# Two blocks in fp32 on one core: slabs of memory on two sets of PSUM banks, the second half of the queries in four steps, and the first layer's memory normalised under the output projection

## The chip, the core and the metric

The kernel runs on one core of one Trainium2 chip, in one launch. The time is device microseconds (us) from the start of the launch to its end, the median of three runs. The engines of the core are TensorE (matmuls, with a separate row PEld for its weight loads), VectorE (DVE), ScalarE (ACT), GpSimd (POOL) and SyncE (SP); each works off its own list of instructions in order. SP's list holds nearly all DMAs, so a DMA that waits for a buffer holds back the DMAs behind it. Matmuls write to PSUM, which has eight banks of 128 x 512 fp32.

## The reference

All tensors are fp32; there are S = 512 positions, a model width of 1024, and 256 rows of memory. Two blocks of two layers each run one after the other. Cut to what the change touches:

```python
for l in range(2):                                   # first block
    mix = concat(diff_attn, mla, sliding_window)(rmsnorm(x, g_mix_pre[l]) @ w_in[l]) @ w_out[l]
    x = x + rmsnorm(mix, g_mix_post[l])
    mem_n = rmsnorm(mem, g_x_mem[l])                 # 256 x 1024
    q = rmsnorm(x, g_x_pre[l]) @ w_xq[l]             # 512 x 1024, four heads of 256
    k, v = split(mem_n @ w_xkv[l], 2)                # 256 x 1024 each
    x = x + rmsnorm(softmax(q k^T / 16) v @ w_xo[l], g_x_post[l])
    x = x + rmsnorm((silu(gate) * up) @ w_ffn_out[l], g_ffn_post[l])

mem_n = rms_norm(mem_2, mem_norm_g)                  # second block, one memory for both layers
for l in range(2):
    x = x + (attention_and_rglru if l == 0 else pool_mixer)(rms_norm(x, mix_norm_g[l]))
    q = rms_norm(rms_norm(x, xattn_norm_g[l]) @ xa_w_q[l], q_g)       # per head of 256
    k, v = split(mem_n @ xa_w_kv[l], 2);  k = rms_norm(k, k_g)
    x = x + softmax(q k^T / 16) v @ xa_w_o[l]
    x = x + square(relu(rms_norm(x, mlp_norm_g[l]) @ mlp_w1[l])) @ mlp_w2[l]
```

## The kernel before

Every fp32 operand is kept as two tiles, H (rounded to the fp32r type) and L (the rest, in the same type), and every product is three matmuls: H by H, H by L, L by H (`three`). Weights come by DMA in chunks of 512 KB into one of three `raw` buffers, ScalarE makes wH and VectorE wL from it (L373, L374 or L371, L429), into a pool `wp` of ten buffers; five chunks fit. Activations are normalised row block by row block: squares and sum on ScalarE (L380), the reciprocal root on POOL, the scaling on VectorE (L406) and ScalarE (L408), four transposes on TensorE (L411) and the split into actH (L347) and actL (L354).

A projection is worked off in slabs of 512 columns. `slab_B` computes rows by columns (tiles pB), `slab_A` the transposed result (tiles pA). A slab takes a named set of PSUM banks: "mm" is the two banks of the pool mm; "A" is mm, mm, tp, tp; "B" is sc, sc, sc, ob; "E", "F" and "K" are other mixtures. The pools hold 2 (mm), 3 (sc), 2 (tp) and 1 (ob) banks, eight in all. A slab's first matmul into a bank waits until the bank's last contents have been read out.

Memory has two row blocks, so a slab of memory needs two banks. Keys are made by `k_first` in the first block (four slabs of 256 columns, one for each head, L371 writes ko) and by `k_second` in the second (two slabs of 512 columns; `head_norm` reads them out: two squares on ScalarE at L832, POOL, two scalings into kn on VectorE at L836; then transposes ktr at L814). Values come from `mem_v`, two slabs (tiles vo). All of them are on "mm". Keys and values go to DRAM and are loaded head by head (xk, xv, L780 and L781) into buffers of `wp`.

The memory of each layer of the first block, and the one memory of the second block, is normalised early by `mem_norm` into tiles memH and memL of the ring r4, stored to DRAM (memd) and loaded again later by `mem_again`. For the first layer this happens in the stage of the input projections (`mem_norm(mem_raw(I["mem"][0]), "xmem0", split[0])`); the tiles are loaded again behind a `hold` on POOL while the attention heads of the layer end, and the output projection w_out (`out_postnorm`, tiles pB from mixH) comes between the reload and `k_first`.

`cross_heads` runs four heads with four units each, one per row block: scores xs on a bank of sc, a maximum on VectorE, the exponential xp on ScalarE (L862), its scaling, two transposes xtr (L869), the split into xpt, and after the fourth unit the outputs xo. In the second block (`second_rest`) the queries are made in two halves of 512 columns; the first half is a slab on "A" ahead of head 0, the second a slab on "B" that `make_q(1)` issues behind unit (0, 1). `make_q` also transposes the queries of its head (ytr, read out into yq).

The order on each engine is set by the tile framework's scheduler, which replays the program with its own costs and places each instruction when its inputs, a buffer and its engine are due; the program order decides between instructions that are ready. So a change in banks or in program order moves instructions over some tens of microseconds around it.

Of the kernel before, what the change touches and what calls it, by code (L numbers as in the profile page):

```python
# [10 lines left out]
F32 = mybir.dt.float32  # L11
# [6 lines left out]
P = 128  # L18
# [136 lines left out]
def two_blocks(ctx: ExitStack, tc: tile.TileContext, I, out):  # L155
# [261 lines left out]
    split = [None]  # L417
    gate = [None]

    def load_chunk(pieces, nk=2, ncols=512, gain=None):  # L420
# [9 lines left out]
        for a in range(nk):  # L430
            split[0] = put_hl(H[:, a], L[:, a], raw[:, a],
                              gain=None if gain is None else gain[:, a:a + 1],
                              copy=gain is not None)
# [325 lines left out]
    def mem_v(act, wkv, vd, tag, halves=(0, 1), t_outer=False, vnew=None):  # L759
        for hf in halves:  # L760
# [14 lines left out]
            slab_B(cols_of(wkv, [(D + hf * 512, D + hf * 512 + 512)]), act, ev, tag, t_outer=t_outer)  # L775
# [9 lines left out]
    def k_first(act, wkv, kv, new, tag="mm"):  # L785
        kd, vd = kv
        for h in range(4):
# [5 lines left out]
            slab_A(cols_of(wkv, [(h * 256, h * 256 + 256)], nk=4), act, ev, tag)  # L793

    def k_second(act, wkv, l, kv, new, tag="mm"):
# [6 lines left out]
        for hf in range(2):  # L802
# [4 lines left out]
            slab_B(cols_of(wkv, [(hf * 512, hf * 512 + 512)]), act, ev, tag)  # L807
# [31 lines left out]
    def cross_heads(make_q, q, kv, kvh, oT, otag="ob"):  # L839
# [6 lines left out]

        def unit(h, t):
            if t == 0 and h + 1 < 4:
                kvh[h + 1] = kv_load(kv, h + 1)
# [110 lines left out]
    def first_layer(l, act, cq, xsrc, nxt_gain, spill, mact, kv, nxt_mem, small):  # L960
# [34 lines left out]
        if mact is None:  # L995
            mact = mem_norm(mem_raw(I["mem"][0]), "xmem0", split[0])

# [358 lines left out]
        mact = mem_again(mact, pt2, marks[(2, 0)])  # L1356
# [14 lines left out]
        mem_v(mact, I["w_xkv"][l], kv[1], "mm")  # L1371
# [76 lines left out]
    def even_layer(act, mact, kv, small):  # L1448
# [133 lines left out]
        mem_v(mact, I["xa_w_kv_2"][0], kv[1], "mm")  # L1582
# [188 lines left out]
```

## Time and profile before

| | us |
|---|---|
| median of 3 runs | 2866.86 (2866.78 to 2867.74) |
| the profiled execution | 2867.16 |
| its span | 2865.4 |
| TensorE busy | 2819.8 (98%) |
| VectorE busy | 1484.6 (52%) |
| ScalarE busy | 1302.0 (45%) |
| GpSimd busy | 206.8 (7%) |

333.56 MB go through the DMAs in the span, 116 GB/s on the mean; 33.16 MB of it are written. The busy time of TensorE counts a matmul from its start to a modelled end, and matmuls overlap; a small idle share can therefore hide in it, and a matmul that takes longer than its like counts as busy as well. How TensorE stands in one stretch is read from its waits, from the granted clock of the stretch, and from the starts of single matmuls.

### The profile page before, as it was taken

To read this page: it belongs to the slowest core of one execution; us is meant where nothing else is said; L and a number is where in the kernel's file an instruction comes from. 1 tells how busy PE (TensorE), PEld (TensorE's weight loads), DVE (VectorE), ACT (ScalarE), POOL (GpSimd) and SP (SyncE) were. 2 spreads that over 40 slices of the span, in tenths; PEclk is the share of its full clock that TensorE was granted. 3 is DMA by queue.
4 is the path that set the end of the run, shared out by engine and by line. 5 is a ranking of instruction groups with operands and counts; after the bars stand their busy time and mean duration, and the time that the engine had idled before them with its cause. 6 is when DMAs were issued, how large, how long until landed. Compare 5 with 4: busy or idle time off the path is not lost.

```text
span 2865.4 us, 39327 instructions
## 1 busy us (share of the span) xinstructions
PE 2819.8 (98%) x14816; PEld 2376.8 (83%) x14816; DVE 1484.6 (52%) x2940; ACT 1302.0 (45%) x2656; POOL 206.8 (7%) x573
## 2 busy tenths in 40 slices
PE   8999999999999999999999999999999999999999
PEld 7868888888898778888888878888888878888887
DVE  7695554334366856543344765555334454554443
ACT  6584444333366745443333664444223344443222
POOL 2121000000011210000000210100000001000000
PEclk9999999999999999999999999999999999999999
DMA  6424633334252345333342523533332353232332
GB/s 206 130 81 138 213 111 96 98 97 131 94 171 88 89 133 184 104 103 97 99 130 95 155 68 119 167 126 97 101 96 96 119 177 110 67 110 96 96 96 74
DMA packets 235645, 333.56 MB, mean 116 GB/s; under 512 B 14656, under 2 KB 135872, under 8 KB 235456
## 3 DMA queue, kind: packets, MB, share of 16 engines
q1 hardware_dynamic: 234880, 328.96, 36.0%
q8 instruction: 116, 1.90, 0.3%
q10 hardware_dynamic: 576, 2.10, 0.2%
q14 instruction: 73, 0.60, 0.1%
HBM read 297.84 MB, written 33.16 MB: 116 GB/s over the span
## 4 chain that ended last, share of the span: by engine, by line
PE 90%; DVE 4%; ACT 4%; issue 1%; DMA 1%; POOL 1%; POOLq 0%; ACTq 0%; DVEq 0%; SPq 0%
PE pB L224 40%; PE pA L224 38%; PE xs L224 2%; PE xo L224 1%; ACT wH L373 1%; PE tr L411 1%; PE ms L224 1%; PE at L1109 1%; ACT h L380 1%; DVE wL L374 1%; PE sws L224 1%; PE mo L224 1%; PE swt L1177 1%; DVE dp L1206 1%; PE dfo L224 1%
## 5 line engine op out<-in xcount | busy, mean ns | idle before, releaser
L374 DVE SCALAR_TENSOR_TENSOR wL<-raw,par,wH 128x512 fp32r<-128x512 f32 (+2 forms) x696 | 436.9, 672 | 505.1 <-ACT wH L373 498.6
L373 ACT ACTIVATE wH<-raw,par 128x512 fp32r<-128x512 f32 (+2 forms) x696 | 417.2, 655 | 592.3 <-issue 216.4
L224 PE MATMUL pA<-actL,wH 128*128 128x512 f32 (+1 forms) x1808 | 650.1, 360 | 0.9 <-DVE actL L354 0.9
L224 PE MATMUL pA<-actH,wH 128*128 128x512 f32 (+1 forms) x1808 | 648.3, 361 | 2.6 <-ACT wH L373 1.5
L224 PE MATMUL pA<-actH,wL 128*128 128x512 f32 (+1 forms) x1808 | 648.0, 360 | 0.4 <-DVE wL L374 0.4
L224 PEld LDWEIGHTS pA<-actH,wH 128*128 128x128 f32 x1808 | 340.6, 189 | 54.8 <-ACT actH L347 1.8
L224 PEld LDWEIGHTS pA<-actH,wL 128*128 128x128 f32 x1808 | 341.5, 189 | 51.0 <-DVE wL L374 0.7
L224 PEld LDWEIGHTS pA<-actL,wH 128*128 128x128 f32 x1808 | 341.9, 189 | 50.4 <-DVE actL L354 1.5
L371 DVE TENSOR_TENSOR wL<-raw,wH 128x512 fp32r<-128x512 f32 (+1 forms) x334 | 215.2, 685 | 324.3 <-ACT wH L429 315.4
L429 ACT CAST wH<-raw 128x1024 fp32r<-128x1024 f32 (+1 forms) x168 | 175.5, 1045 | 338.6 <-PE pB L224 160.5
L224 PE MATMUL pB<-wL,mH 128*128 128x512 f32 x512 | 199.2, 389 | 0.0
L224 PE MATMUL pB<-wH,mH 128*128 128x512 f32 x512 | 198.8, 389 | 0.0
L224 PE MATMUL pB<-wH,mL 128*128 128x512 f32 x512 | 198.8, 389 | 0.0
L224 PE MATMUL pB<-wH,actH 128*128 128x512 f32 (+2 forms) x416 | 143.4, 349 | 2.2 <-ACT xp L862 1.5
L224 PE MATMUL pB<-wL,actH 128*128 128x512 f32 (+2 forms) x416 | 144.2, 347 | 0.4 <-DVE wL L374 0.4
L224 PE MATMUL pB<-wH,actL 128*128 128x512 f32 (+2 forms) x416 | 144.0, 347 | 0.0
L224 PE MATMUL pB<-wL,fH 128*128 128x512 f32 x352 | 137.5, 391 | 0.0
L224 PE MATMUL pB<-wH,fL 128*128 128x512 f32 x352 | 136.5, 390 | 0.0
L224 PE MATMUL pB<-wH,fH 128*128 128x512 f32 x352 | 136.2, 390 | 0.0
L224 PEld LDWEIGHTS pB<-wH,mH 128*128 128x128 f32 x512 | 96.1, 188 | 20.1
L224 PEld LDWEIGHTS pB<-wH,mL 128*128 128x128 f32 x512 | 96.1, 188 | 20.0
L224 PEld LDWEIGHTS pB<-wL,mH 128*128 128x128 f32 x512 | 96.1, 188 | 19.8
(361 smaller groups left out, 4666.4 us busy)
## 6 DMA issues: line engine op xcount, KB each, us to landing
raw<-in_mlp_w SPq DMA_DIRECT2D x128, 512.0 KB, 3.7
raw<-in_w_ffn_in SPq DMA_DIRECT2D x176, 256.0 KB, 3.2
raw<-in_w_ffn_out SPq DMA_DIRECT2D x44, 512.0 KB, 3.4
raw<-in_w_xkv SPq DMA_DIRECT2D x32, 512.0 KB, 4.1
raw<-in_xa_w_kv SPq DMA_DIRECT2D x32, 512.0 KB, 4.4
raw<-in_ev_w_in SPq DMA_DIRECT2D x20, 512.0 KB, 3.7
raw<-in_w_in SPq DMA_DIRECT2D x16, 512.0 KB, 4.9
raw<-in_w_out SPq DMA_DIRECT2D x16, 512.0 KB, 3.6
```

The source lines that it names most:

```text
L224: nc.tensor.matmul(o, a, b, start=start, stop=stop_)
L371: nc.vector.tensor_tensor(out=l, in0=src, in1=h.bitcast(F32), op=ALU.subtract)
L373: i = nc.scalar.activation(h, src, AF.Copy, scale=gain)
L374: nc.vector.scalar_tensor_tensor(out=l, in0=src, scalar=gain, in1=h.bitcast(F32), op0=ALU.mult, op1=ALU.subtract)
L380: nc.scalar.activation(junk, src, AF.Square, scale=1.0 / 32.0, accum_out=ssq[:, hf:hf + 1])
L411: nc.tensor.transpose(pt[:, i * P:(i + 1) * P], h[j][:, i * P:(i + 1) * P], ident)
L429: nc.scalar.copy(H, raw)
L1109: nc.tensor.transpose(tp[:, i * P:(i + 1) * P], src[:, i * P:(i + 1) * P], ident)
L1177: nc.tensor.transpose(tp[:, i * P:(i + 1) * P], pr[i][:, kt * P:(kt + 1) * P], ident)
L1206: nc.vector.tensor_tensor_reduce(out=pm[m], in0=sc, in1=ndt[t], scale=-DIFF_SLOPES[h], scalar=BIG, op0=ALU.add, op1=ALU.min, accum_out=nmx)
```

## The change

There are three parts. First, slabs of memory alternate between the sets "mm" and "B": the heads of `k_first`, the halves of `k_second`, and the halves of `mem_v` where both are made together (in the last layer each half of the values is still alone, on "mm").

Second, the first layer's memory is no longer normalised among the input projections. Its two raw tiles of 512 KB are loaded behind a `hold` on the marker at which the reload stood before, and `mem_norm` writes the normalised halves straight into tiles of the pool ptp (`new=pt2`). There is no copy in DRAM for this layer: four writes of 512 KB and eight reads of 256 KB go. A tile of ptp holds two column blocks instead of four, so the split takes four instructions per row block on ScalarE and four on VectorE instead of two and two with the double size, as before on reloading. The other two memories keep their way through DRAM. The helper that tied the first memory's squares to a weight conversion (`split`, `issue_after`) goes.

Third, the second half of the queries in the second block is issued in four steps of 24 matmuls on "mm": the first two row blocks over chunks 0 and 1, then over chunks 2 and 3, then the other two row blocks over the same chunks, which stay in `wp` until then. One step follows each unit of head 0. The keys and values of head 1 are loaded in unit (0, 3) instead of (0, 0).

```diff
-    def mem_raw(memrow):
+    def mem_raw(memrow, after=None):
         ms = [r4([P, D], F32, "memraw") for _ in range(MEM // P)]
         for t, m in enumerate(ms):
+            hold(m, after)
             nc.sync.dma_start(out=m, in_=memrow[t * P:(t + 1) * P, :])
         return ms

-    def mem_norm(ms, name, after=None):
-
-        act = Act(8, MEM, "mem", gain=pr(name), new=r4)
+    def mem_norm(ms, name, new=r4):
+
+        act = Act(8, MEM, "mem", gain=pr(name), new=new)
         for t, m in enumerate(ms):
-            h = [hbuf([P, S], F32, "h") for _ in range(2)]
-            ssq = sm(3, "ssq")
-            with tc.issue_after(after) if after is not None else nullcontext():
-                sq_halves(m, h, ssq)
-            prenorm_tile(m, act, t, "tp", ssq, h)
+            prenorm_tile(m, act, t, "tp")
+        if new is not r4:
+            return act
         act.copy = drp.tile([2, 8, P, MEM], F32, name=nm("memd"))
...
-            slab_B(cols_of(wkv, [(D + hf * 512, D + hf * 512 + 512)]), act, ev, tag, t_outer=t_outer)
+            slab_B(cols_of(wkv, [(D + hf * 512, D + hf * 512 + 512)]), act, ev,
+                   ("mm", "B")[hf] if len(halves) == 2 else "mm", t_outer=t_outer)
...
-            slab_A(cols_of(wkv, [(h * 256, h * 256 + 256)], nk=4), act, ev, tag)
+            slab_A(cols_of(wkv, [(h * 256, h * 256 + 256)], nk=4), act, ev, ("mm", "B")[h % 2])
...
-            slab_B(cols_of(wkv, [(hf * 512, hf * 512 + 512)]), act, ev, tag)
+            slab_B(cols_of(wkv, [(hf * 512, hf * 512 + 512)]), act, ev, ("mm", "B")[hf])
...
-            if t == 0 and h + 1 < 4:
+            if t == (3 if parts and h == 0 else 0) and h + 1 < 4:
                 kvh[h + 1] = kv_load(kv, h + 1)
...
                 for t in range(NT):
                     yield unit(h, t)
+                    if h == 0 and parts:
+                        yield piece(parts[t])
                     if t == 1 and h + 1 < 4:
                         yield filler(h + 1)
...
-        if mact is None:
-            mact = mem_norm(mem_raw(I["mem"][0]), "xmem0", split[0])
-
...
-        mact = mem_again(mact, pt2, marks[(2, 0)])
+        if mact is None:
+            mact = mem_norm(mem_raw(I["mem"][0], marks[(2, 0)]), "xmem0", pt2)
+        else:
+            mact = mem_again(mact, pt2, marks[(2, 0)])
         load_x(xsrc, marks[(2, 2)])
...
+        def quarters():
+
+            nrm = nrms[1] = [r2([P, S], F32, "yn") for _ in range(NT)]
+            src, n = cols_of(wq, [(512, 1024)])
+            ch, banks = {}, {}
+
+            def step(p, c):
+                if c == 0:
+                    banks[p] = banks_of("mm", 2, "pB")
+                for kc in (2 * c, 2 * c + 1):
+                    if kc not in ch:
+                        ch[kc] = src(kc, act2.gain)
+                    H, L = ch[kc]
+                    for i in range(2):
...
+                            three(banks[p][i], H[:, k2, :], L[:, k2, :], act2.h(k, *ts),
+                                  act2.l(k, *ts), k == 0, k == act2.nk - 1, False)
+                if c == 1:
+                    for i in range(2):
+                        head_norm(banks[p][i], nrm[2 * p + i], 2, 256)
+
+            return [lambda p=p, c=c: step(p, c) for p in range(2) for c in range(2)]
+
         def make_q(h):
             hf = h // 2
-            if h < 2:
-                slab_q(h)
+            if h == 0:
+                slab_q(0)
...
-        cross_heads(make_q, q, kv, kvh, oT, "mm")
+        cross_heads(make_q, q, kv, kvh, oT, "mm", quarters())
```

Three places show what this does to the order. On TensorE, at the keys of the last layer (`k_second`), the list before has these rows; pB_21374 and pB_21375 are the two banks of the first half of the keys, pB_21474 is the first bank of the second half, and ktr is the transposed first half:

```order
L224 MATMUL pB_21375<-wH_21438,memH_21040 128x512
L224 MATMUL pB_21375<-wL_21439,memH_21040 128x512
L224 MATMUL pB_21375<-wH_21438,memL_21041 128x512
L814 MATMUL ktr_21574<-csb,kn_21370 128x128
L224 MATMUL pB_21474<-wH_21478,memH_21038 128x512
L224 MATMUL pB_21474<-wL_21479,memH_21038 128x512
L224 MATMUL pB_21474<-wH_21478,memL_21039 128x512
```
and the changed list, where pB_21359 and pB_21360 are the first half and pB_21459 the first bank of the second:

```order
L224 MATMUL pB_21360<-wH_21423,memH_21025 128x512
L224 MATMUL pB_21360<-wL_21424,memH_21025 128x512
L224 MATMUL pB_21360<-wH_21423,memL_21026 128x512
L224 MATMUL pB_21459<-wH_21463,memH_21023 128x512
L224 MATMUL pB_21459<-wL_21464,memH_21023 128x512
L224 MATMUL pB_21459<-wH_21463,memL_21024 128x512
L224 MATMUL pB_21459<-wH_21463,memH_21023 128x512
```
Before, a transpose of the first half's keys stands between the halves, and the second half begins in a bank of the same pair. Now the second half begins right behind the first, in other banks; its 48 matmuls follow without a break and the transposes come behind them.

On TensorE, at head 0 of the cross attention of the second block's first layer, before (ytr are query transposes, xs the scores of one row block each, pB the second half of the queries on four banks, of which pB_17895 is the first):

```order
L1668 MATMUL ytr_17843<-csb,yn_17663 128x128
L1668 MATMUL ytr_17843<-csb,yn_17664 128x128
L1668 MATMUL ytr_17843<-csb,yn_17665 128x128
L224 MATMUL xs_17856<-xk_17658,yq_17834 128x256 x2
L224 MATMUL xs_17871<-xk_17658,yq_17834 128x256 x2
L224 MATMUL pB_17895<-wH_17901,actH_17090 128x512
L224 MATMUL pB_17895<-wL_17902,actH_17090 128x512
L224 MATMUL pB_17895<-wH_17901,actL_17091 128x512
```
and now (pB_17857 is the second of the two banks of the first row blocks, and wH_17940 the last weight chunk):

```order
L224 MATMUL pB_17857<-wH_17940,actH_17077 128x512
L224 MATMUL pB_17857<-wL_17941,actH_17077 128x512
L224 MATMUL pB_17857<-wH_17940,actL_17078 128x512
L224 MATMUL xs_17841<-xk_17643,yq_17823 128x256 x2
L224 MATMUL xs_17903<-xk_17643,yq_17823 128x256 x2
L224 MATMUL xs_17999<-xk_17643,yq_17823 128x256 x2
L224 MATMUL xs_17841<-xk_17643,yq_17824 128x256
L224 MATMUL xs_17841<-xk_17643,yq_17823 128x256 x2
L224 MATMUL xs_17903<-xk_17643,yq_17824 128x256
```
Before, two scores begin when few matmuls of the second half are done, and one bank of it after the other is finished behind them. Now half of the second half, 48 matmuls over all four chunks, is finished ahead of the scores, and three scores begin together.

On ScalarE, among the first input projections, before (memraw is the first layer's memory, wH_364 and wH_667 are weights, actH the input):

```order
L347 CAST actH_131<-tr_216 128x4x128
L373 ACTIVATE wH_364<-raw_362,par 128x512 x2
L380 ACTIVATE h_514,ssq_516<-memraw_506 128x512
L380 ACTIVATE h_515,ssq_516<-memraw_506 128x512
L380 ACTIVATE h_540,ssq_542<-memraw_507 128x512
L380 ACTIVATE h_541,ssq_542<-memraw_507 128x512
L373 ACTIVATE wH_667<-raw_664,par 128x416 x2
L347 CAST actH_129<-tr_234 128x4x128
```
and now:

```order
L347 CAST actH_129<-tr_208 128x4x128
L373 ACTIVATE wH_364<-raw_362,par 128x512 x2
L347 CAST actH_131<-tr_216 128x4x128
L373 ACTIVATE wH_602<-raw_599,par 128x416 x2
L347 CAST actH_129<-tr_234 128x4x128
L347 CAST actH_131<-tr_242 128x4x128
L698 ACT_TABLE_LOAD
```
The four squarings of memory are gone from between the two weights. They now stand at the end of the layer's attention, ahead of the output projection's first read-outs.

## Rows read from the trace of the kernel before

**Rows 1.** The page: span, and the chain that ended last, by engine.
```profile
span 2865.4 us, 39327 instructions
...
PE 90%; DVE 4%; ACT 4%; issue 1%; DMA 1%; POOL 1%; POOLq 0%; ACTq 0%; DVEq 0%; SPq 0%
```

**Rows 2.** Chain, 1960 to 2070: start us, us, engine tile line and count.
```profile
...
2001.62 43.52 PE pB L224 x192
...
```

**Rows 3.** Stretches: us, busy (count) of PE, PEld, DVE, ACT, POOL; PEclk, DMA, GB/s.
```profile
...
57.00:80.00 23.00, 20.75 (x149) 19.75 (x147) 17.71 (x43) 16.03 (x50) 7.66 (x25) 0.93 0.64 202
213.00:244.00 31.00, 29.68 (x192) 23.09 (x187) 8.50 (x18) 4.92 (x10) 3.32 (x10) 1.00 0.39 140
...
270.00:321.00 51.00, 49.06 (x314) 45.13 (x313) 36.38 (x71) 34.12 (x75) 4.71 (x10) 0.97 0.71 224
1805.00:1854.00 49.00, 49.00 (x227) 40.74 (x226) 26.26 (x43) 24.97 (x53) 4.52 (x10) 1.00 0.67 222
2305.00:2345.00 40.00, 37.13 (x164) 29.99 (x163) 24.98 (x43) 23.84 (x53) 4.79 (x10) 0.96 0.62 198
...
```

**Rows 4.** TensorE by time: start us, us, line, instruction [idle before <-releaser].
```profile
...
2316.75 0.39 PE L224 MATMUL pB<-wH,memL 128*128 128x512 f32 x1
2319.86 0.33 PE L814 MATMUL ktr<-csb,kn 128*128 128x128 f32 x1 [2.72 <-DVE kn L836]
2320.34 0.47 PE L224 MATMUL pB<-wH,memH 128*128 128x512 f32 x1 [0.15 <-DVE kn L836]
...
2322.23 0.63 PE L224 MATMUL pB<-wH,memH 128*128 128x512 f32 x1
...
```

**Rows 5.** ScalarE by time, first of four squarings of memory.
```profile
...
21.33 0.62 ACT L380 ACTIVATE h<-memraw 128x512 f32<-128x512 f32 x1
...
```

**Rows 6.** TensorE's waits, 20 to 28: waited for, us in total, times, longest.
```profile
...
PE pB L224 <- ACT wH L373: 0.7, 1, 0.7
PE pB L224 <- DVE wL L374: 0.4, 1, 0.4
...
```

**Rows 7.** The same, 57 to 80.
```profile
...
PE sws L224 <- ACT krot L1044: 1.6, 1, 1.6
PE ltr L1021 <- DVE memL L354: 0.6, 1, 0.6
```

**Rows 8.** Chain, 56 to 80: four transposes.
```profile
...
57.39 0.44 PE tr L411 x4
...
```

**Rows 9.** TensorE's waits, 240 to 270.
```profile
...
PE pB L224 <- ACT mixH L370: 0.7, 1, 0.7
PE mo L224 <- ACT pt L1126: 0.6, 1, 0.6
```

**Rows 10.** The same, 270 to 321.
```profile
...
PE tr L411 <- DVE h L406: 1.9, 1, 1.9
```

**Rows 11.** The same, 800 to 830.
```profile
...
PE tr L411 <- DVE actL L354: 1.2, 1, 1.2
PE pA L224 <- DVE ko L371: 0.9, 1, 0.9
```

**Rows 12.** The same, 1590 to 1624.
```profile
...
PE pA L224 <- ACT wH L373: 1.5, 1, 1.5
PE pB L224 <- DVE kn L836: 0.5, 1, 0.5
```

**Rows 13.** The same, 1854 to 1918.
```profile
...
PE xtr L869 <- DVE xpt L371: 0.8, 1, 0.8
PE pB L224 <- ACT xp L862: 0.8, 1, 0.8
PE xo L224 <- ACT xpt L370: 0.6, 1, 0.6
...
```

**Rows 14.** Tile xk: idle before its readers, and landing of its loads.
```profile
...
  ACT yq L370: 2.2, 8
...
DMA to landing us min/median/max: 3.9/5.0/7.5
```

More of the change, by code (lines that the diff above doesn't have):

```diff
@@ L415, in prenorm_tile @@
         norm_halves(src, lambda j, p3: act.put(4 * j, t, p3), tag, ssq, h)
-    split = [None]
     gate = [None]
@@ L430, in load_chunk @@
         for a in range(nk):
-            split[0] = put_hl(H[:, a], L[:, a], raw[:, a],
-                              gain=None if gain is None else gain[:, a:a + 1],
-                              copy=gain is not None)
+            put_hl(H[:, a], L[:, a], raw[:, a],
+                   gain=None if gain is None else gain[:, a:a + 1], copy=gain is not None)
         return H, L
@@ L757, in k_out, with mem_v @@
         return put
-    def mem_v(act, wkv, vd, tag, halves=(0, 1), t_outer=False, vnew=None):
+    def mem_v(act, wkv, vd, halves=(0, 1), t_outer=False, vnew=None):
         for hf in halves:
@@ L783, in kv_load, with k_first @@
         return k, v
-    def k_first(act, wkv, kv, new, tag="mm"):
+    def k_first(act, wkv, kv, new):
         kd, vd = kv
@@ L791, in ev, with k_second @@
                 put(g, bank[:, :MEM])
-            slab_A(cols_of(wkv, [(h * 256, h * 256 + 256)], nk=4), act, ev, tag)
-    def k_second(act, wkv, l, kv, new, tag="mm"):
+            slab_A(cols_of(wkv, [(h * 256, h * 256 + 256)], nk=4), act, ev, ("mm", "B")[h % 2])
+    def k_second(act, wkv, l, kv, new):
         kd, vd = kv
@@ L837, in head_norm, with cross_heads @@
                                     r[:, h:h + 1], None, op0=ALU.mult)
-    def cross_heads(make_q, q, kv, kvh, oT, otag="ob"):
+    def cross_heads(make_q, q, kv, kvh, oT, otag="ob", parts=()):
         pts = {}
@@ L845, in filler, with piece @@
             yield
+        def piece(f):
+            f()
+            yield
         def unit(h, t):
-            if t == 0 and h + 1 < 4:
+            if t == (3 if parts and h == 0 else 0) and h + 1 < 4:
                 kvh[h + 1] = kv_load(kv, h + 1)
@@ L1370, in first_layer @@
             k_first(mact, I["w_xkv"][l], kv, r4)
-        mem_v(mact, I["w_xkv"][l], kv[1], "mm")
+        mem_v(mact, I["w_xkv"][l], kv[1])
         oT = Act(8, S, "xo")
@@ L1581, in even_layer @@
         out_residual([cols_of(wo, [(0, 512)]), cols_of(wo, [(512, 1024)])], mix, [2, 3, 0, 1], nx)
-        mem_v(mact, I["xa_w_kv_2"][0], kv[1], "mm")
+        mem_v(mact, I["xa_w_kv_2"][0], kv[1])
         where[0] = pt2
@@ L1626, in odd_layer @@
         where[0] = p2
-        mem_v(mact, I["xa_w_kv_2"][1], kv[1], "mm", (0,), vnew=pt2)
+        mem_v(mact, I["xa_w_kv_2"][1], kv[1], (0,), vnew=pt2)
         act2, nx = next_norm("xa1")
@@ L1638, in odd_layer @@
             nx(t, None, None)
-        mem_v(mact, I["xa_w_kv_2"][1], kv[1], "mm", (1,), vnew=pt2)
+        mem_v(mact, I["xa_w_kv_2"][1], kv[1], (1,), vnew=pt2)
         where[0] = pt2
@@ L1656, in slab_q @@
             slab_B(cols_of(wq, [(hf * 512, hf * 512 + 512)]), act2, ev, "AB"[hf])
+        def quarters():
[10 more added lines that the diff above has]
+                    for i in range(2):
+                        ts = (2 * p + i) * P, (2 * p + i + 1) * P
+                        for k2 in range(src.nk):
+                            k = kc * src.nk + k2
+                            three(banks[p][i], H[:, k2, :], L[:, k2, :], act2.h(k, *ts),
[4 more added lines that the diff above has]
+            return [lambda p=p, c=c: step(p, c) for p in range(2) for c in range(2)]
         def make_q(h):
             hf = h // 2
-            if h < 2:
-                slab_q(h)
+            if h == 0:
+                slab_q(0)
             nrm = nrms[hf]
```

## The prediction

> **What bounds the kernel now.** I read the chain of waits first. TensorE holds 90% of it, VectorE and ScalarE 4% each, in a span of 2865.4 us [rows 1]. So the end moves only where TensorE stands still or runs slowly; work taken from another engine or from the DMAs counts only if TensorE was waiting for it. A matmul of 512 columns inside a dense stretch starts every 43.52 / 192 = 0.227 us [rows 2]. Next I listed TensorE's waits stretch by stretch in the stretches that the change touches, and the table of stretches for the granted clock [rows 3]. Last came single instructions around the longest pause. The profiled execution took 2867.16 us, 1.76 more than its span and 0.30 more than the median of the runs shown, 2866.86; the sum is made against 2867.16.
>
> A pause is a little longer than the idle time that the views print. At the longest one the last matmul starts at 2316.75 and the next instruction at 2319.86 [rows 4]: 3.11, less its own step of 0.227, is 2.88, where the view prints 2.72. I add 0.16 us for each pause that closes.
>
> **Memory of the first layer.** What goes from the start: four squarings of 512 columns on ScalarE between 21.33 and 23.78 us [rows 5], and with them two waits of TensorE for weights, 0.7 and 0.4 us [rows 6], because in order on ScalarE the weight conversion stands behind the squarings. Bounds 0 to 1.1; I take **1.1**, since nothing else is between them.
>
> From the stage at 57 to 80 us go four casts, four subtractions, 16 transposes and the writes to DRAM. TensorE waits there 1.6 us for krot and 0.6 us for memL, which holds the bank of the next transposes [rows 7]. Behind these two the granted clock is 0.93 of full over 23 us [rows 3], which is a spell at 1.2 GHz instead of 2.4 and costs 23 x 0.07 = 1.6. Together 3.8. The second wait goes with the instruction that made it. The first has two copies of swak in front of krot as well as a cast of memH, and only the cast goes; I leave 0.8 of it. Taken **3.0**, bounds 0 to 3.8.
>
> The work comes back between 213 and 244 us, where ScalarE is busy for 4.92 of 31 us and VectorE for 8.50 [rows 3]: that idle time hides the squarings, casts and subtractions. The new form splits the casts in two, eight instead of four, and that is hidden by the same idle time; without that cover the squarings alone would put 4 x 0.62 = 2.5 us ahead of the output projection's weights on ScalarE. The 16 transposes come at 0.44 us for four [rows 8], 1.8 in all, that leave 57 to 80 and land beside two waits of 0.7 and 0.6 us [rows 9]. They fill these, so moving them is worth **1.3** (bounds -1 to 1.3: they could be late and delay the first keys). The reload from DRAM and its eight DMAs go from SP's queue; no wait of TensorE in the rows ends on them, so that is 0. The two raw loads, 512 KB each, are queued on SP ahead of x and behind the first chunk of the output weights, and the layer's first use of memory is 60 us later.
>
> **Two sets of banks for the slabs of memory.** Before, every slab of keys takes the two banks of the same pair, so its first matmul waits until the slab before it has been read out. At 270 to 321 us TensorE waits 1.9 us once [rows 10] and the clock is 0.97 over 51 us [rows 3], 1.5 more: 3.4; I take **3.0**, since ScalarE and VectorE are busy for 34 and 36 of the 51 us and leave less room than elsewhere. At 800 to 830: 1.2 + 0.9 = 2.1 [rows 11], taken **1.8**. At 1590 to 1624: 1.5 + 0.5 = 2.0 [rows 12], taken **1.8**; the first of these waits is for a weight of the next projection, which the scheduler had put there only as filling, and the second half of the keys now stands in its place. At 2305 to 2345: 2.72 + 0.15 behind kn [rows 4], which is the read-out of the first half of the keys, and eight matmuls of which one takes 0.63 instead of 0.39: the clock over the stretch is 0.96 of 40 us [rows 3], 1.6. Together 4.5, and I take all of it, since 96 matmuls stand in a row now where the read-out was waited for; its one condition, the weights of the second half, is the matter of the first rival. Bounds of each are 0 and its full price. The value slabs get two sets as well, but TensorE is busy for 49.00 of 49 us at 1805 to 1854 [rows 3]: 0.
>
> **Second half of the queries in four steps.** In each layer of the second block TensorE waits 0.8 + 0.8 + 0.6 = 2.2 us while the heads run [rows 13]; the layer at 2410 shows the same waits. In the new order 48 matmuls of the second half stand ahead of the first score, and the scores of all four row blocks of head 0 find matmuls beside them: 4.4 in all. Two costs are added. The queries of head 1 are transposed three matmuls before their first score, and scores wait 2.2 us for yq in eight places now [rows 14], so one more such wait is about 0.3. And k of head 1 is loaded into a buffer that the fifth weight chunk held. From the last matmul on that chunk to the first score there are 21 matmuls of 512 columns, 3 of 256 and 8 transposes: 21 x 0.227 + 3 x 0.12 + 8 x 0.11 = 6.0 us. A load of k lands in 3.9 to 7.5 us, median 5.0 [rows 14]: no wait at the median, 1.5 at the worst; I take 0.4. Behind that load on SP stand v and the next k, which are wanted later. So 2 x (2.2 - 0.3 - 0.4) = **3.0**, bounds -3 to 4.4.
>
> **Sum.** 1.1 + 3.0 + 1.3 + 3.0 + 1.8 + 1.8 + 4.5 + 3.0 = 19.5. Some 17 pauses close, 17 x 0.16 = 2.7. The order of the sliding-window and other attention heads of layer 0 is shuffled as well, with dense matmuls on both sides; no row prices that, and I put it at 0 with 2 us either way, but allow for two new waits of the size of the largest in the heads, 2 x 0.8 = 1.6. Gain 19.5 + 2.7 - 1.6 = 20.6: 2867.16 - 20.6 = **2846.6**. If every pause closes in full it is 1.1 + 3.8 + 1.3 + 3.4 + 2.1 + 2.0 + 4.5 + 4.4 = 22.6, with 19 x 0.16 = 3.0 and the 2 of the shuffle 27.6: 2839.6.
>
> **Rivals.**
>
> *The banks give nothing: weights and read-out are the pace.* Then the bank terms (3.0 + 1.8 + 1.8 + 4.5 and 7 x 0.16 = 12.2) stay and 8.4 is left: 2858.8. For it: around the keys ScalarE and VectorE are each busy for 60 to 71% and the DMAs for 62 to 71% of 51 and 40 us [rows 3], and one of the waits named is for a weight. Against it: at 1805 to 1854 slabs of the same weights run with no idle at all at the same DMA share. Two rules of the Trainium skill stand on its side, both from "TensorE: Matmul & The Clock Gate". Its section "HAM oscillation — how this bites in real kernels" tells of a matmul kernel in which a second set of PSUM buffers brought no further gain once the contraction ran through; by it the time would be this rival's. Its section "A second HAM failure mode: psum-queue depth-cycling" says that cycling through PSUM banks can make the engine idle for moments that bring the slower clock back. By that, a spell of 1.6 us at each of seven pairs of slabs would cost 11.2 of the 20.6: 2857.8. No row bears the second out: the clock is 1.00 at 1805 to 1854, where slab follows slab [rows 3].
>
> *The pauses only move.* The matmuls that filled a gap are missing further on, where ScalarE or VectorE are still converting. Then only the part that takes work away is left, 1.1 + 3.0 + 1.3 = 5.4: 2862. For it: VectorE is at 36 of 51 us in the first of these stretches. Against it: the pauses are read-outs of about 3 us, and beside them stands a whole half slab, 24 matmuls of 5.4 us.
>
> *Slower: the late loads of k.* k, v and the next k go out in one burst behind three chunks of output weights. If these six of 512 KB shared the 222 GB/s of rows 3, k would land after 6 x 0.52 / 222 = 14.2 us, and TensorE would stand still for 8.2 us and run slowly for 1.6 behind it, in both layers: 19.6 lost, and the 3.0 gone: 2869.2; with the bank terms gone as well 2881. It decides from a landing over 6.0 us on, and turns the sign at about 14. Against it: the worst of 16 loads of k took 7.5, under the load of now.
>
> **How the numbers follow.** About 0.2% (5.7 us) is what a measurement of this kernel can tell from no change. Forecast 0.66; banks give nothing 0.20; pauses move 0.09; late loads 0.05. The forecast's own range is 2839.6 to 2854. The range for 8 in 10 takes in most of the second case: 2838 to 2860. Faster by over 0.2% (under 2861): the forecast and most of the second case, 0.84. Within: the third case, a little of the second and half of the last, 0.12. Slower: 0.04.
>
> **What would show it.** Right: no wait of TensorE over 1 us between two key slabs in any of the four places; the granted clock at 1.00 in 2305 to 2345 and near it in 270 to 321; no krot or memL wait at the start; four scores of head 0 among matmuls of the query projection. A wait of the first score of head 1 that ends on the load of k shows the last term too small. Wrong: a gap that ends on wH or wL inside the second key slab (second case), or waits of the old size a few us further on (third).

## The result and the profile after

The changed kernel takes 2842.31 us (median of 4 runs, 2841.95 to 2843.09), the kernel before 2867.30 in the runs beside it: 25.0 us less, a ratio of 0.9913 with a 95% interval of 0.9896 to 0.9930. The forecast was 2846.6 with a range of 2838 to 2860. One of all the executions behind the times of this document, of the variant with one piece on mm below, took 3700.26 us at a granted clock of 0.71 and stays out of its ratio. The page of the profile after shows the span and who holds the chain, to be read against [rows 1]:

```profile
span 2840.9 us, 39283 instructions
...
PE 93%; DVE 3%; ACT 3%; issue 1%; POOL 0%; DMA 0%; POOLq 0%; ACTq 0%; DVEq 0%; SPq 0%
...
```

TensorE's share of the chain grew from 90 to 93%: what went was time in which the chain had passed through VectorE, ScalarE, GpSimd and the DMAs.

Since TensorE executes the same 14816 matmuls and transposes in both profiles, the gain can be laid over the program. The following table is worked out from the two traces: the start of an instruction after less its start before, as the median over the instructions of a stretch, read where both kernels have executed the same matmuls again (from 57 to 240 us but for the 16 transposes of memory, which stand later now). Times are those of the kernel before.

| stretch, us | what runs there | forecast | measured |
|---|---|---|---|
| 0 to 40 | first projections | 1.1 | 1.5 |
| 40 to 110 | projections and first heads, without 16 transposes | 3.0 + 1.8 | 1.2 |
| 110 to 170 | attention heads | 0 | 2.0 |
| 170 to 220 | attention heads, end | 0 | -0.4 |
| 220 to 260 | output projection, with the 16 transposes | -0.5 | -0.6 |
| 260 to 360 | keys and values of layer 0 | 3.0 | 4.4 |
| 780 to 860 | keys of layer 1 | 1.8 | 2.9 |
| 1060 to 1120 | values of layer 1 | 0 | 0.9 |
| 1560 to 1640 | keys, third layer | 1.8 | 2.4 |
| 1820 to 1900 | heads, third layer | 1.5 | 2.4 |
| 2280 to 2360 | keys, last layer | 4.5 | 4.8 |
| 2360 to 2460 | heads, last layer | 1.5 | 2.4 |

With the forecast's 2.7 for the underread pauses and its allowance of 1.6 the forecast column makes 20.6; the measured one makes 23.9, and 0.3 lies between these stretches. Two profiled executions stand behind the column, and where the kernel before has a spell at the lower clock in its own (around 68, 280 and 2321 us) the row depends on that spell, by 1.5 us at the first keys; the last section shows this.

The stretches by engine in the changed kernel (columns as in [rows 3]; the same work stands up to 24 us earlier than there):

```profile
...
20.00:28.00 8.00, 8.00 (x68) 8.00 (x67) 6.44 (x19) 4.98 (x9) 0.00 (x0) 1.00 0.70 193
57.00:80.00 23.00, 20.93 (x157) 20.36 (x156) 14.50 (x46) 16.36 (x48) 3.61 (x14) 0.93 0.35 94
220.00:262.00 42.00, 41.99 (x246) 33.38 (x245) 18.41 (x34) 18.52 (x43) 3.87 (x12) 1.00 0.17 51
264.00:315.00 51.00, 51.00 (x333) 46.78 (x332) 38.82 (x78) 36.87 (x84) 6.19 (x12) 1.00 0.75 238
1790.00:1839.00 49.00, 49.00 (x228) 40.83 (x227) 27.96 (x46) 26.83 (x56) 4.21 (x9) 1.00 0.63 213
2283.00:2323.00 40.00, 40.00 (x186) 33.25 (x185) 28.31 (x47) 27.39 (x59) 5.96 (x12) 1.00 0.61 192
...
```

At the first keys (264 to 315) and at the last (2283 to 2323) TensorE is busy without a gap and the clock is 1.00, where [rows 3] had 49.06 of 51 at 0.97 and 37.13 of 40 at 0.96. ScalarE and VectorE do more in the same stretch (36.87 instead of 34.12, 38.82 instead of 36.38): they had room. At 57 to 80 nothing like that happened: 0.93 before, 0.93 after.

The loss of 0.4 at the end of the heads (in the table, 170 to 220) goes back to the second part. ScalarE by time (start us, us, instruction, idle before and its releaser) shows a chunk of the output weights that lands late in the changed kernel, and the read-out pt, for which TensorE then waits 0.3 us, is queued behind it:

```profile
...
204.68 1.05 ACT L428 CAST wH<-raw 128x1024 fp32r<-128x1024 f32 x1 [2.35 <-DMA raw<-in_w_out]
205.63 0.58 ACT L1127 COPY pt<-at 128x512 f32<-128x512 f32 x1
...
```

The kernel before waited 0.42 us for such a chunk there. The two raw loads of memory now stand on SP's queue between the first chunk of these weights and the others; that they are the reason was not tested, but the other two kernels with the second part lose 0.5 and 0.6 us at the same place.

The longest pause of before [rows 4] stood between the halves of the last layer's keys. The chain of waits of the changed kernel over that stretch (start us, us, what) shows one piece of 182 matmuls across it, with the transposes behind:

```profile
...
2269.80 41.26 PE pB L224 x182
2311.06 0.88 PE ktr L812 x8
...
```

In the heads of the third layer the waits of 0.8, 0.8 and 0.6 us [rows 13] have become these (TensorE waited for, us in total, times, longest):

```profile
...
PE pB L224 <- DVE yoL L371: 0.6, 2, 0.3
PE xo L224 <- DVE yn L834: 0.3, 1, 0.3
```

No wait on the late load of k is among them. The view of tile xk, against [rows 14], shows all 16 loads slower on the median and one more wait for yq:

```profile
...
  ACT yq L370: 3.2, 9
...
DMA to landing us min/median/max: 3.9/5.5/8.7
```

The late load itself is not one of the slow ones. The same view for the k of head 1 alone (third layer, issued at 1857.5):

```profile
...
DMA to landing us min/median/max: 3.9/3.9/3.9
```

In the last layer it is 4.0. This load is the first of its burst; those of heads 2 and 3, issued behind it, took 6.7 and 8.7 us in the third layer.

### The profile page after: what moved, and what is told of

Same layout as the page of the kernel before. It is cut to its first block, busy times and chain, and to the rows that moved or that the text cites. A ratio compares the mean times of both kernels' runs of the same rounds, so it can differ in the third digit from the quotient of the medians.

```text
span 2840.9 us, 39283 instructions
## 1 busy us (share of the span) xinstructions
PE 2812.2 (99%) x14816; PEld 2375.3 (84%) x14816; DVE 1484.1 (52%) x2944; ACT 1300.3 (46%) x2660; POOL 206.8 (7%) x567
## 4 chain that ended last, share of the span: by engine, by line
PE 93%; DVE 3%; ACT 3%; issue 1%; POOL 0%; DMA 0%; POOLq 0%; ACTq 0%; DVEq 0%; SPq 0%
PE pB L224 42%; PE pA L224 39%; PE xs L224 2%; PE xo L224 2%; PE tr L411 1%; PE at L1110 1%; PE ms L224 1%; PE dfo L224 1%; ACT wH L373 1%; PE swt L1178 1%; PE mo L224 1%; PE swo L224 1%; PE sws L224 1%; DVE dp L1207 1%; PE po L224 0%
```

## The experiments

**Each part alone.** Three kernels take the kernel before and one part of the change each; a fourth takes the new sets for the keys of the second block alone. The kernel before was timed again beside each group of kernels and has medians from 2865.07 to 2868.10 there, so differences of one or two us between kernels of different groups rest on the traces. The first part:

```diff
-            slab_B(cols_of(wkv, [(D + hf * 512, D + hf * 512 + 512)]), act, ev, tag, t_outer=t_outer)
+            slab_B(cols_of(wkv, [(D + hf * 512, D + hf * 512 + 512)]), act, ev,
+                   ("mm", "B")[hf] if len(halves) == 2 else tag, t_outer=t_outer)
...
-            slab_A(cols_of(wkv, [(h * 256, h * 256 + 256)], nk=4), act, ev, tag)
+            slab_A(cols_of(wkv, [(h * 256, h * 256 + 256)], nk=4), act, ev, ("mm", "B")[h % 2])
...
-            slab_B(cols_of(wkv, [(hf * 512, hf * 512 + 512)]), act, ev, tag)
+            slab_B(cols_of(wkv, [(hf * 512, hf * 512 + 512)]), act, ev, ("mm", "B")[hf])
```

> The kernel before with the first part alone (slabs of memory alternate between the sets mm and B). Theory: each pause between two key slabs closes by itself, whatever the rest does. The changed kernel reached the end of the four stretches earlier by 3.6 (first keys), 2.9 (second layer's keys), 3.1 and 4.8 us (keys of the second block): 14.4 in all, so about 2853. Rival: weights and read-out are the pace and the new order of the other parts made the gain: 2863 or more. Rival: the first keys gained because memory no longer comes from DRAM: 10.8 instead of 14.4, 2856.5.

Measured: 2851.84 us, ratio 0.9948 (0.9936 to 0.9961), 14.45 less than the 2866.29 beside it. The theory stands, both rivals fall; that the 14.4 fits to the tenth is chance. Laid over the program the gains are 3.6 and 0.7 around the first keys and values, 2.9 at the keys of layer 1, 0.9 at its values, 2.4 and 5.1 at the keys of the second block, 15.6 in all: the third layer's keys brought less than the 3.1 taken, and the values brought 1.6 that nobody had taken.

Of these three edits, the last alone:

> The kernel before with the two sets for the keys of the second block alone (k_second; first block and values as before). Theory: 3.1 + 4.8 = 7.9 us: 2859.4, and the granted clock at 1.00 in the last layer's keys. Rival (the pace is weights and read-out): the wait of 2.7 us becomes one for wH or wL and less than 3 us come: 2864.3 or more.

Measured: 2859.64, ratio 0.9976 (0.9966 to 0.9985), 6.65 less; over the program 2.4 to 2.5 at the one place and 4.5 to 5.1 at the other. The rival falls, and the pauses between the key slabs close there whatever the rest of the kernel does.

The third part alone (the last line of its edit; `quarters`, the steps behind the units and the later load are as in the change):

```diff
...
-        cross_heads(make_q, q, kv, kvh, oT, "mm")
+        cross_heads(make_q, q, kv, kvh, oT, "mm", quarters())
```

> The kernel before with the third part alone (second half of the queries in four steps on mm). Theory: 2.4 us in each of the two layers, 4.8 in all: 2862.5, with no wait for the load of k of head 1. Rival: it needs the other sets for memory to be free of pauses around it: under 1 us, 2866.5 or more. Rival, late load of k: slower than before.

Measured: 2863.16, ratio 0.9984 (0.9975 to 0.9993), 3.13 less; over the program 2.4 in each of the two layers. The theory of 2.4 in each layer stands by the traces, and both rivals fall; the difference of the medians is less than its 4.8.

The second part alone (the calls; `mem_raw` and `mem_norm` are as in the change):

```diff
-            mact = mem_norm(mem_raw(I["mem"][0]), "xmem0", split[0])
...
+            mact = mem_norm(mem_raw(I["mem"][0], marks[(2, 0)]), "xmem0", pt2)
```

> The kernel before with the second part alone (first layer's memory normalised under the output projection, no DRAM). Theory: worth 1.5 us at the start, about 1 at 57 to 80, 2 in the attention of the first layer, less some 0.6 under the output projection: 4 in all, 2863.3, and the pause of 1.9 us at the first keys stays. Rival: the first keys gain with it, another 3.6: 2859.7. Rival: the gain in the attention belongs to the other parts' order: 2865.3.

Measured: 2863.13, ratio 0.9991 (0.9982 to 1.0000), 3.16 less. The total fits the theory, though it is hardly clear of no change and does not tell the theory from the last rival; the trace does, for this kernel gains 1.6 at 110 to 170 us by itself. But its lead does not last: over the program it is ahead by 4.4 at 260 us (the changed kernel by 3.7), by 2.6 at 320 and by 1.5 at 860. TensorE's waits at 235 to 345 in this kernel say where the first 1.9 went:

```profile
...
PE tr L411 <- DVE h L406: 2.7, 1, 2.7
PE pA L224 <- DVE ko L371: 0.9, 1, 0.9
...
```

The pause of 1.9 us at the first keys [rows 10] has grown to 2.7, and one of 0.9 behind ko has come. With one pair of banks the time gained ahead of the keys is waited away at them. The other 1.0, at the keys of layer 1, is another matter. The waits there are those of the kernel before (1.1 and 0.9 against 1.2 and 0.9 [rows 11]), but the granted clock over 790 to 835 us is 0.96 where the kernel before had 1.00:

```profile
...
790.00:835.00 45.00, 42.97 (x300) 40.36 (x299) 33.74 (x66) 30.23 (x73) 9.43 (x20) 0.96 0.63 200
...
```

**Parts in company.** Apart, the three parts take 14.45 + 3.16 + 3.13 = 20.7 us off; together 25.0. The changed kernel without its third part (the edit against it, in short):

```diff
-            if h == 0:
-                slab_q(0)
+            if h < 2:
+                slab_q(h)
...
-        cross_heads(make_q, q, kv, kvh, oT, "mm", quarters())
+        cross_heads(make_q, q, kv, kvh, oT, "mm")
```

> The first and second part together, without the four steps. Apart the parts took off 14.45 and 3.16 us, the steps 3.13, together 20.7, where all three took off 25.0: some 4 us come only in company. Theory: memory alone brings the layer's keys forward into a longer pause (2.7 instead of 1.9 us at the first keys) and loses there what it gained before; with two sets it keeps it. Then these two together give 19 to 20.5: 2846.5 to 2848 against 2867, and the steps keep 4 to 5 for the rest. Rival: the surplus is between the steps and the banks: 17.6 here, 2849.5. Rival: the surplus is the spread between chips: 17 to 21, with no change in the waits at the first keys.

Measured: 2846.86, ratio 0.9928 (0.9915 to 0.9942), 21.2 less than the 2868.10 beside it. Over the program it is ahead by 3.6 at 260 and 10.9 at 860, as the changed kernel is (3.7 and 11.0). From 260 to 860 it gains 7.3 us, as the banks alone do (7.2), where memory alone loses 2.9. So most of the surplus is between memory and banks: the gain of the second part survives the keys if these have two sets. The 4.5 us to the changed kernel are the steps, 2.4 in each layer as alone; alone their medians showed only 3.13 of it. How much of the 4.3 is that, and how much the difference between the groups of runs, stays open.

**Is it the steps that pay?** Three variants of the third part in the changed kernel. First, the four steps in a row ahead of head 0, with k and v of head 1 loaded in unit (0, 0) as before:

```diff
-            if t == (3 if parts and h == 0 else 0) and h + 1 < 4:
+            if t == 0 and h + 1 < 4:
...
             make_q(0)
+            for f in parts:
+                f()
             for h in range(4):
...
-                    if h == 0 and parts:
-                        yield piece(parts[t])
```

> The changed kernel with the four steps issued one after the other ahead of head 0 (k and v of head 1 loaded in unit (0, 0) again). Theory: what pays in the steps is that matmuls stand beside the scores of head 0; with them ahead the units wait for maximum, exponential and split again, 1 to 2.4 us in each of the two layers: 2844.5 to 2847. Rival: what pays is the order of the contraction (two row blocks at a time, no slab on four banks) wherever it stands: 2842.3, same.

Measured: 2843.02, ratio 0.9916 (0.9903 to 0.9930). The rival holds on the time, but not as it was put: in the trace the scheduler has 18 matmuls of the scores (three row blocks) ahead of the last 48 by itself. So a second variant keeps one piece at its old place, behind unit (0, 1), on mm in two passes:

```diff
-                    if h == 0 and parts:
-                        yield piece(parts[t])
...
             if h == 0:
                 slab_q(0)
+            elif h == 1:
+                for f in parts:
+                    f()
```

> The changed kernel with the second half of the queries in one piece at its old place behind unit (0, 1), but on the banks mm in two passes as now. Theory: what the steps took away is the slab on B, whose banks sc are those of the scores, so that units (0, 2), (0, 3) and head 1 had to wait for its read-out; on mm they need not, and one piece keeps the gain: 2842.3 to 2843.5. Rival: what pays is that one step follows each unit: half of the steps' 4.5 us is lost, 2844.5 or more.

Measured: 2842.84, ratio 0.9921 (0.9908 to 0.9935). The steps as such pay nothing: one piece does as well, with waits in other places (TensorE's waits in the third layer's heads):

```profile
...
PE xo L224 <- DVE xpt L371: 1.0, 1, 1.0
PE xs L224 <- ACT yq L370: 0.5, 1, 0.5
PE xtr L871 <- DVE yq L371: 0.4, 1, 0.4
```

The reason is that TensorE's order is the scheduler's and not the program's. TensorE by time (start us, us, instruction) has nearly the same order in the changed kernel, in the first variant and in the second, one line of each: 48 matmuls of the second half, then three scores together, then the rest.

```profile
...
1848.46 2.32 PE L224 MATMUL xs<-xk,yq 128*128 128x256 f32 x18
...
```

```profile
...
1848.62 2.31 PE L224 MATMUL xs<-xk,yq 128*128 128x256 f32 x18
...
```

```profile
...
1848.65 2.31 PE L224 MATMUL xs<-xk,yq 128*128 128x256 f32 x18
...
```

What these three have in common against the kernel before is the pair mm in the place of set B, three of whose four banks are those of the scores, and with it two passes of two row blocks each. The two were not taken apart (one pass on four banks that the scores do not use was not tried). For the banks speaks one wait of before, 0.8 us of a matmul of the queries for xp, which reads a score [rows 13]. In all of them, and in the next variant, the load of k of head 1 goes out at the same time (1857.5 to 1858.1 us), whichever unit asks for it. The third variant is the first again, with the scores of head 0 held behind the last of the 96 matmuls:

```diff
+            with tc.issue_after(behind[0]) if behind[0] is not None and h == 0 else nullcontext():
...
+            behind[0] = lastmm[0].ins if parts else None
```

> As whole_first, but the scores of head 0 are issued behind the last matmul of the second half, where whole_first left the scheduler free to put 13 of them among these matmuls. Theory of the banks: 2842.5 to 2843.5. Rival (matmuls beside the scores are what pays): the first transposes of head 0 and the queries of head 1 wait for exponential and split, 1 to 2.4 us in each of the two layers: 2844.5 to 2847, with waits of TensorE for xp or xpt in head 0.

Measured: 2852.75, ratio 0.9953 (0.9939 to 0.9966): 10.4 us slower than the changed kernel, 5.3 in each layer over the program. Now all four scores stand in one piece behind the 96 matmuls:

```profile
...
1862.23 3.25 PE L226 MATMUL xs<-xk,yq 128*128 128x256 f32 x24
...
```

That costs more than the rival had put down, and the waits in the third layer, with the stretch by engine, say why:

```profile
...
PE pB L226 <- DVE yn L836: 1.7, 1, 1.7
PE xtr L875 <- DVE xp L871: 1.4, 1, 1.4
PE xs L226 <- ACT yq L372: 0.9, 1, 0.9
...
```

```profile
...
1860.00:1870.00 10.00, 7.78 (x47) 6.79 (x46) 5.92 (x18) 5.52 (x16) 1.44 (x2) 0.93 1.05 352
...
```

The cover works both ways. The transposes of head 0 wait for xp (1.4), as the rival said; but the second pass of the queries also waits 1.7 us for the read-out of its own two banks, which the scores had covered, and a spell at the lower clock follows (0.93 over these 10 us). So scores and matmuls must stand among each other; that the banks of the scores must be free as well is likely but not shown by itself.

**The values.**

```diff
-                   ("mm", "B")[hf] if len(halves) == 2 else "mm", t_outer=t_outer)
+                   "mm", t_outer=t_outer)
```

> The changed kernel with both halves of the values on mm, as before. Theory: the values had no wait before, so the second set is worth nothing there: 2842.3, within 1 us. Rival: with the pauses at the keys gone the values are next and wait for their bank: 1 to 3 us slower, with a wait of TensorE between the two halves of the values.

Measured: 2844.08, ratio 0.9921 (0.9907 to 0.9934), 1.8 us over the changed kernel in medians, which the times alone do not tell from no change. By the traces the theory holds in the second block, where nothing changed, and fails in the first. Its waits at 285 to 335 us:

```profile
...
PE xs L224 <- ACT xq L373: 0.5, 1, 0.5
```

and at 1055 to 1105:

```profile
...
PE pB L224 <- DVE vo L371: 0.2, 1, 0.2
```

The changed kernel has no wait in either. Laid over the program the loss is 1.1 us in layer 0 and 0.9 in layer 1; the banks alone gained 0.7 and 0.9 there. The rival's amount is right, its wait between the two halves is not: that is 0.2 us in layer 1 and nothing in layer 0, and where the rest is lost stays open.

**Why 57 to 80 did not gain.** In the changed kernel TensorE waits there for these:

```profile
...
PE pB L224 <- ACT vt L1066: 1.1, 1, 1.1
PE sws L224 <- DVE nmx L1152: 1.0, 1, 1.0
```

ScalarE by time shows a weight chunk that lands late, with ckv and vt queued behind its conversion:

```profile
...
60.97 1.71 ACT L373 ACTIVATE wH<-raw,par 128x256 fp32r<-128x256 f32 x4 [1.23 <-DMA raw<-in_w_in]
62.58 0.35 ACT L373 ACTIVATE ckv<-ltr,par 128x128 fp32r<-128x128 f32 x1
62.83 0.25 ACT L1043 COPY vt<-pB 128x128 f32<-128x128 f32 x1
...
```

A chunk's load waits until VectorE is through with an earlier chunk in one of the three raw buffers, as the waits of SP's queue at 30 to 75 us show (line, waited for, us in total, times, longest):

```profile
...
SPq L423 <- DVE wL L374: 9.8, 5, 6.2
...
```

Two kernels give one or four chunks of this place a tile of the ring r4 instead:

```diff
-        raw = rawp.tile([P, nk, ncols], F32, tag="raw", name=nm("raw"))
+        if spare[0]:
+            spare[0] -= 1
+            raw = r4([P, nk, ncols], F32, "raw")
+        else:
+            raw = rawp.tile([P, nk, ncols], F32, tag="raw", name=nm("raw"))
```

> The changed kernel, with one weight chunk of the first layer (the first of the first differential slab) loaded into a tile of the ring r4 instead of the third raw buffer. In the changed kernel ScalarE waits 1.23 us for that kind of chunk at 60.97 us, with the split of ckv and the read-out of vt queued behind it, and TensorE then waits 1.0 and 1.1 us and runs at 0.61 of full clock over 66 to 70. Theory: the raw buffers are the pace there, since a chunk's load waits until VectorE is through with an earlier one; with a spare buffer up to 2.1 + 1.6 us come back: 2838.6 to 2841. Rival: the read-outs themselves are the pace, 2842.3, same.

> As spare1, but four chunks take tiles of r4: both of the compressed-query slab and both of the first differential slab. The read-outs of ckv, swak and vt then stand ahead of the weight conversions on ScalarE. Theory (raw buffers are the pace): 2838.6 to 2840.5. Rival (read-outs are the pace): 2842.3.

Measured: 2847.76 (ratio 0.9931, 0.9917 to 0.9944) and 2844.49 (0.9923, 0.9910 to 0.9935): 5.4 and 2.2 us slower than the changed kernel. The stretches of the changed kernel:

```profile
...
60.00:66.00 6.00, 3.92 (x30) 3.52 (x30) 5.12 (x15) 4.68 (x16) 1.70 (x6) 1.00 0.93 258
66.00:70.00 4.00, 4.00 (x24) 4.00 (x23) 1.35 (x4) 0.55 (x2) 1.51 (x8) 0.61 0.10 29
...
80.00:100.00 20.00, 19.55 (x135) 17.64 (x134) 13.34 (x43) 10.62 (x37) 4.27 (x12) 1.00 0.19 58
...
```

and of the kernel with one spare buffer:

```profile
...
60.00:66.00 6.00, 6.00 (x53) 6.00 (x52) 4.60 (x15) 3.33 (x11) 3.22 (x12) 1.00 0.53 146
66.00:70.00 4.00, 4.00 (x36) 4.00 (x35) 0.00 (x0) 0.37 (x1) 0.00 (x0) 1.00 0.00 0
...
80.00:100.00 20.00, 17.49 (x107) 13.32 (x106) 11.97 (x41) 8.69 (x27) 2.44 (x8) 0.83 0.06 16
...
```

The theory is right on the place and wrong on the sum, and so is its rival. The pauses at 60 to 66 and the spell at 66 to 70 are gone, so the raw buffer was their cause; but TensorE now waits at 80 to 100 for lat and pt (1.5 and 1.0) and runs at 0.83, perhaps because the matmuls that ran late are missing there:

```profile
...
PE ltr L1027 <- DVE lat L1024: 1.5, 1, 1.5
PE swt L1184 <- DVE pt L1135: 1.0, 1, 1.0
```

Behind that, from 105 to 245 us, its waits sum to 4.2 us, against 1.7 in the changed kernel; 1.8 of them are for pt, in three places. With four spare buffers the same two waits stand at 80 to 100 at full clock. That kernel falls behind the changed one only between 100 and 240 us, by 1.3 by then; why is open.

## Why the prediction was right, and where it was mis-sized

The mechanism of the largest terms, the keys, is shown. Part of the good total is luck all the same: at 57 to 80 us nothing of 3.0 came, and the attention heads behind it, the values and the cross heads gave 5.4 us more than their terms.

**Start (1.1).** 1.5 measured; the changed kernel has no wait of TensorE at 20 to 28 us. Right.

**57 to 80 (3.0).** Wrong. By 110 us only 1.2 had come, less than the 1.8 of the 16 transposes that left, so nothing is left for this term; the other two kernels with the second part show 1.6. The step that failed is that krot and memL would be followed by nothing: two waits of 1.1 and 1.0 took the place of 1.6 and 0.6 [rows 7], and the spell at the lower clock stayed. Behind the memory's instructions on ScalarE stood a chunk of weights, and that is what the rows of ScalarE, read by time, could have shown beforehand. This is the rival of the moved pauses, true of this one stretch, and the spare buffers show how it goes on.

**Shuffled heads of layer 0 (0, with 2 us either way).** 2.0 came at 110 to 170 us, 1.6 and 1.5 in the other two kernels with the second part. TensorE's waits there fell from 2.0 to 0.9 us, which is half of it. No term had a reason for it, so this is luck.

**Transposes under the output projection (1.3).** Right where they land: -0.6 against -0.5 by the sum, and the waits of [rows 9] are gone. The raw loads were put at no cost; a late weight chunk behind them, with 0.4 us at 210, was overlooked.

**Keys (3.0, 1.8, 1.8, 4.5).** Mechanism right, shown by the part alone and by the keys of the second block alone; sizes small: 3.6, 2.9, 2.4 and 4.8. I had cut the terms of the stretches where VectorE and ScalarE looked full, and they were not. The spells at the first keys and at the last went with the pauses: in all nine profiles of kernels with two sets for all keys the granted clock is 1.00 around the keys of all four layers. But their price, 1.5 and 1.6, was read from one execution of the kernel before, and not every execution has them there. The forecast's first rival falls with it. What the Trainium skill tells in "TensorE: Matmul & The Clock Gate", "HAM oscillation — how this bites in real kernels", of a kernel in which a second set of PSUM buffers gave no further gain, does not carry over to this one: the second set alone is worth 14.45 us. Nor does the section "A second HAM failure mode: psum-queue depth-cycling" of the same page of the Trainium skill, by which cycling through banks can bring the slower clock: with more sets in turn the granted clock rose, from 0.97 and 0.96 at the first and last keys to 1.00.

**Values (0).** Wrong by 1.6 us in the first block (banks alone, over the program; 1.8 in the medians of the changed kernel without it). The row of 1805 to 1854 is of the second block only; I carried it over to slabs that I had not looked at.

**Heads (3.0).** 4.8. The two costs were put too high. k of head 1 had 6.0 us to land and took 3.9 and 4.0: it goes out first in its burst, so the median of all loads was the wrong row for it, and the third rival, in which six loads share their rate equally, falls with that. The 2.2 us in eight places for yq [rows 14] were misread: by time they are all idle time of the weight loads (PEld), and no score matmul of before waited over 0.15 us for yq; after, one does, for 0.16. The reason was half right: that matmuls stand beside the scores matters, as the strict order shows, but the four steps do not bring it about; pair mm with its two passes does.

**Reading of pauses (2.7) and new waits (-1.6).** The first cannot be measured by itself; the keys gave 2.6 more than their terms, of which it would be 1.1. For the second, new waits came where nothing was put down (57 to 80), and in the heads only three of 0.3.

Together the terms were 4.3 us short of the 24.9 between 2867.16 and 2842.31: key slabs, values and cross heads gave about 6 more than their terms and the heads of layer 0 gave 2, while 57 to 80 us gave 3.6 less, counting the transposes. The signs that were to show it came: no wait between key slabs, the clock, scores among matmuls, and no krot or memL wait, the last one by its letter only.

## What to carry to other kernels

A slab that takes the banks of the slab before it can cost its read-out (0.5 to 2.7 us at the keys here, nothing at the values of the second block), and banks shared with another user (here the scores) may cost waits as well; giving the next slab other banks is cheap where the matmuls behind it are ready. Before a stall is put down as gone, read by time what else is queued on the engine that released it: the next in its queue may be as late. And time gained ahead of a stage that waits for something else is lost there, so parts that look independent should be tried in company. A spell at the lower clock that one profile shows should not be priced as if every execution had it.

## What was not expected of the hardware

The clock does not follow from the pause alone. Up to the second block the kernel before and the one with new sets for the second block's keys alone run the same instructions, and TensorE waits alike: 1.9 us at the first keys in both [rows 10], 1.2 and 0.9 at those of layer 1 in both [rows 11]. The kernel before has a clock of 0.97 at the first [rows 3] and 1.00 at the second:

```profile
...
790.00:835.00 45.00, 42.83 (x298) 39.57 (x297) 36.21 (x72) 31.91 (x78) 9.64 (x21) 1.00 0.60 190
...
```

In the other it is the reverse:

```profile
...
270.00:321.00 51.00, 49.06 (x322) 44.92 (x321) 36.98 (x72) 35.21 (x78) 4.93 (x11) 1.00 0.75 232
790.00:835.00 45.00, 42.97 (x292) 40.05 (x291) 35.49 (x70) 31.17 (x76) 9.67 (x21) 0.96 0.60 188
...
```

Over the program that gives it 1.5 us at the one place and costs it 1.1 at the other, for the same pauses. Memory alone has the pause at the last layer's keys too (2.5 us), at a clock of 1.00 where the kernel before had 0.96. It fits that kernels with such pauses spread more from run to run: 26 runs of the kernel before on one chip lie between 2863.45 and 2869.73 us, 11 of memory alone between 2860.65 and 2869.54, but five of the banks alone between 2851.06 and 2852.19 and four of the changed kernel within 1.2 us. It is not so for all: five of memory and banks, which have no pause at the keys, spread over 3.4 us. That the spells are the reason for the spread was not shown.
